# A new order for a four-layer encoder: finer tracking of writes, copies of three heads' outputs, and an earlier guard for the last projection

## The chip, the cores and the metric

The kernel runs on one core of one Trainium2 chip. The metric is device time in microseconds, from the start of the program to its end. It was run three times before the change; the profiled execution is a further one, and its trace shows each instruction on the core's engines: TensorE (PE, with its weight loads PEld), VectorE (DVE), ScalarE (ACT), GpSimd (POOL) and SyncE (SP), which issues the transfers.

## The reference

The program is a trunk of four layers over 512 rows of 1024 channels, all in float32. Each layer normalizes its input, mixes the rows in one of three ways, multiplies by a gate, projects and adds to the input. All mixing is causal by chunks of 64 rows.

```python
for i in range(DEPTH):                     # DEPTH = 4
    kind, j = i % N_MIXERS, i // N_MIXERS  # 0, 1, 2, 0
    h = _rms_norm(x, norm_g[j])
    x = x + mixer[kind](h, ...)

def _diff_attention(h, w_in, ...):         # layers 0 and 3
    q, k, v, gate = jnp.split(h @ w_in, ...)
    # 8 heads; q and k in two maps of 64, normalized and rotated; v of 128
    wts = p[:, :, 0] - lam * p[:, :, 1]    # two softmaxes, chunk-causal
    o = _rms_norm(wts @ v, sub_g) * (1.0 - lambda_init)
    return (o * silu(gate)) @ w_out

def _conformer_conv(h, w_in, ...):         # layer 1
    a, b, gate = jnp.split(h @ w_in + b_in, 3, axis=-1)
    u = a * sigmoid(b)
    u = causal_depthwise_conv(u, conv_w) + conv_b      # 31 taps
    u = silu(_layer_norm(u, ln_g, ln_b))
    return (u * silu(gate)) @ w_out

def _mla(h, w_in, ...):                    # layer 2: latent attention, 8 heads
    ...
    return (o * silu(gate)) @ w_out
```

## The kernel before

**Tiling.** Rows are four tiles of 128, channels eight blocks of 128. A product of full precision is three matmuls: both operands are split in a high and a low part, and the names `Hh`, `Hl` are the two parts of the layer's normalized input. A projection holds accumulators of 128 x 512 in PSUM and runs over eight blocks of the contracted channels, whose weights arrive in four pieces (`g1_w0`, `w2`, `w4`, `w6`). Names begin with the layer (`L0_` to `L3_`; the profile shows `L_` for all): `qk`, `v`, `g` are projections, of which `g0` and `g1` make the two halves of the gate `G`; `h5j2` is head 5, query tile 2, with its scores `sc`, its exponentials `p`, their transposes `wtr` and copies `wt`; `o5` is head 5's output.

**The attention of layers 0 and 3** (`layer_a`). For each head and query tile TensorE makes scores, VectorE their maxima, ScalarE the exponentials; VectorE combines the two maps; TensorE transposes the result and multiplies it with V, into the head's accumulator `po`. Then ScalarE squares the output (`osq`), small operations make the factor of the norm, and `gate_o` (VectorE, L526) multiplies output, factor and gate into `V`. Only after that is `po` free. The gate must have gone through Silu, one ScalarE instruction over 128 x 2048 per half, and Silu and Exp stand in different function tables (`ACT_TABLE_LOAD`). Afterwards `ytr` transposes `V` blockwise, and ScalarE and VectorE split it into the high and low part of `y`.

**The convolution of layer 1** (`layer_b`). Blocks of channels are convolved in two ways. Blocks 0 to 4 run as multiply-and-add steps on VectorE (block 4's are the rows `L1_c4`) or on ScalarE and GpSimd (`cq`, `ct`, `cs`), and TensorE transposes the sums (`ctr`). Blocks 5 to 7 run on TensorE (`L1_c5` to `L1_c7`): `conv_phase` fills a tile `u4` of 128 x 4 x 136 by a memset of margins and sixteen transfers of 32 rows each, and VectorE expands weights (`wa5` to `wa7`, four pieces a block). Then the LayerNorm: statistics of all blocks on VectorE (L547, L550), the root on GpSimd (`lnr_y`, L740), the normalization into `V` (L535), the transposes `ytr`.

**The output projection** (`out_proj`) multiplies `y` with its weights `o0_w`, `o1_w`. In the last layer it begins each accumulator with transposes of the residual `X` (L468 before, L472 after), which a guard, `only_when`, holds back until a named `y` is written.

**What sets the order.** The kernel's methods do not issue instructions. They describe nodes for a planner (class `Plan`), each with an engine, a cost, the buffers it reads and writes, and a place in the program. The planner then simulates the five engines and takes for each the node that could start first; among those that could, the lowest priority number, which is the node's place plus an entry of the table `SHIFT` for its section and engine. It also gives out buffer slots: four for projection accumulators, three for scores and transposes, one for `po` (tag `o`), and in SBUF four of 128 x 512 for scratch (tag `mid`). What depends on what inside the planner is tracked per buffer in grains (`Buf.grain` elements of a row) and parts of the 128 rows (`View.halves`). The order that comes out is issued as it stands, each engine in its own queue, and the waits on the chip are set by the tiles that the instructions touch.

## Time and profile before

| what | value |
|---|---|
| three runs | 1047.22, 1045.62, 1047.05 us (median 1047.05) |
| profiled execution, its own time | 1047.38 us |
| span of its trace | 1045.6 us, 1.8 us less |
| mean granted TensorE clock | 0.99 |
| PE busy | 1006.7 us (96%) |
| DVE busy | 762.4 us (73%) |
| ACT busy | 585.1 us (56%) |
| POOL busy | 194.8 us (19%) |
| DMA | 87.53 MB, mean 84 GB/s |

A row of the slices names the stretch, its length, and each engine's busy time with the number of instructions, then the granted clock of TensorE (1.00 is full speed), the busy share of the DMA engines and GB/s. A row of the waits says which engine waited at which line for what: total, times and longest. A row of the timeline gives start, duration, engine, line and operation, output and inputs, how many instructions of the kind follow one another, and in brackets the idle time ahead of it with what ended it.

### The profile page before, as it was taken

The page shows a single profiled execution, that of the slowest core. Times are in us where ns is not written, and L with a number is a line of the kernel's source. Part 1 is how long each engine was busy: PE and PEld are TensorE (multiplying, and loading weights), DVE is VectorE, ACT ScalarE, POOL GpSimd, SP SyncE. Part 2 cuts the span into 40 slices and gives each one's busy share as a digit, 9 for nine tenths or more (in the row PEclk, how much of TensorE's full clock was granted, in tenths as well). Part 3 has the DMA queues.
Part 4 walks back from the last instruction along what each step waited for, and adds up shares of the span by engine and source line. Part 5 has one row for each costly group of instructions (what it writes and reads, how often), then busy time and mean ns, then how long its engine had stood idle before and what let it go on. Part 6 is the DMA issues. An engine that isn't in the chain of part 4 may idle for free.

```text
span 1045.6 us, 15204 instructions
## 1 busy us (share of the span) xinstructions
PE 1006.7 (96%) x5204; PEld 846.2 (81%) x5204; DVE 762.4 (73%) x1970; ACT 585.1 (56%) x1222; POOL 194.8 (19%) x135
## 2 busy tenths in 40 slices
PE   9999999999999999997999998999999999999798
PEld 7878888787877787886888788788888887887687
DVE  4946899896678999847353869964776589889660
ACT  7437557657444656554343676753526555765742
POOL 3000000000130898950520001000400000000000
PEclk9999999999999999998999999999999999999899
DMA  7343244222124333220232211013325124323002
GB/s 235 93 101 122 61 122 121 66 87 56 41 61 121 122 89 101 66 90 1 73 83 78 71 50 61 22 39 101 119 72 152 38 84 121 102 81 120 22 21 81
DMA packets 74308, 87.53 MB, mean 84 GB/s; under 512 B 17109, under 2 KB 47701, under 8 KB 74232
## 3 DMA queue, kind: packets, MB, share of 16 engines
q1 hardware_dynamic: 74232, 86.57, 28.1%
q8 instruction: 41, 0.67, 0.3%
q14 instruction: 35, 0.29, 0.1%
HBM read 75.28 MB, written 2.10 MB: 74 GB/s over the span
## 4 chain that ended last, share of the span: by engine, by line
PE 72%; DVE 14%; ACT 6%; issue 4%; POOL 2%; DMA 1%; SPq 0%; DVEq 0%; ACTq 0%; POOLq 0%
PE L_o L460 20%; PE L_g_a L460 14%; PE L_qk_a L460 12%; PE L_v_a L460 8%; DVE L_c L526 4%; PE L_ab_a L460 2%; PE L_c_a L460 1%; POOL L_cq L517 1%; PE L_c L460 1%; DVE L_qk_T L514 1%; PE L_qk_tr L466 1%; ACT G L490 1%; PE L_kv_a L460 1%; DVE L_qk_t L514 1%; PE L_h3j_sc L460 1%
## 5 line engine op out<-in xcount | busy, mean ns | idle before, releaser
L460 PE MATMUL L_qk_a<-L_qk_w,Hh 128*128 128x512 f32 x512 | 161.6, 397 | 0.0
L460 PE MATMUL L_o<-L_y,L_o_w 128*128 128x512 f32 x576 | 141.6, 395 | 0.0
L460 PE MATMUL L_g_a<-L_g_w,Hh 128*128 128x512 f32 x384 | 121.4, 397 | 2.3 <-ACT L_qk_sq L490 1.9
L460 PEld LDWEIGHTS L_o<-L_y,L_o_w 128*128 128x128 f32 x576 | 105.2, 188 | 21.1 <-POOL L_o_w L517 0.4
L740 POOL TENSOR_TENSOR L_h_or_y<-L_h_ov,minus_half 128x4 f32<-128x4 f32 x16 | 17.4, 1089 | 484.3 <-DVE L_h_ov L535 311.7
L460 PEld LDWEIGHTS L_qk_a<-L_qk_w,Hh 128*128 128x128 f32 x512 | 92.5, 188 | 16.8 <-ACT G L490 0.3
L460 PE MATMUL L_qk_a<-L_qk_w,Hl 128*128 128x512 f32 x256 | 100.5, 392 | 0.6 <-DVE Hl L526 0.6
L517 POOL TENSOR_TENSOR L_cq<-L_cq,L_ct 128x512 f32<-128x512 f32 x58 | 80.2, 1382 | 27.9 <-DMA L_ab_w_r<-b_w_in 21.3
L460 PE MATMUL L_ab_a<-Hh,L_ab_w 128*128 128x512 f32 x256 | 81.6, 393 | 3.0 <-DVE L_ab_sg L514 2.1
L460 PEld LDWEIGHTS L_g_a<-L_g_w,Hh 128*128 128x128 f32 x384 | 69.6, 188 | 16.6 <-ACT L_qk_sq L490 2.3
L460 PE MATMUL L_v_a<-L_v_w,Hh 128*128 128x512 f32 x256 | 81.0, 397 | 0.7 <-DVE L_qk_t L514 0.5
L460 PE MATMUL L_g_a<-L_g_w,Hl 128*128 128x512 f32 x192 | 75.2, 391 | 0.0
L526 DVE SCALAR_TENSOR_TENSOR L_c<-L_u,L_tab,L_c 128x512 f32<-128x512 f32 x90 | 65.0, 750 | 1.4
L490 ACT ACTIVATE L_ct<-L_u,L_tab 128x512 f32<-128x512 f32 x60 | 42.6, 721 | 33.3 <-POOL L_cq L517 31.6
L460 PEld LDWEIGHTS L_ab_a<-Hh,L_ab_w 128*128 128x128 f32 x256 | 47.9, 188 | 15.4 <-DVE L_ab_sg L514 2.0
L460 PEld LDWEIGHTS L_qk_a<-L_qk_w,Hl 128*128 128x128 f32 x256 | 48.0, 188 | 11.9 <-DVE Hl L526 1.7
L460 PEld LDWEIGHTS L_v_a<-L_v_w,Hh 128*128 128x128 f32 x256 | 46.2, 188 | 9.9 <-DVE L_qk_t L514 1.0
L517 POOL TENSOR_TENSOR L_sqs<-L_sqs,L_sq 128x512 f32<-128x512 f32 x21 | 32.1, 1528 | 98.3 <-ACT L_sq L490 84.5
L514 DVE TENSOR_TENSOR L_g_w<-L_g_w_r,L_g_w 128x1024 fp32r<-128x1024 f32 x32 | 43.9, 1374 | 8.8 <-ACT L_g_w L497 8.2
L460 PE MATMUL L_v_a<-L_v_w,Hl 128*128 128x512 f32 x128 | 50.1, 391 | 0.0
L460 PE MATMUL L_ab_a<-Hl,L_ab_w 128*128 128x512 f32 x128 | 49.9, 390 | 0.0
L497 ACT CAST L_o_w<-L_o_w_r 128x1024 fp32r<-128x1024 f32 x32 | 33.6, 1052 | 28.7 <-PE L_g_a L460 16.4
(368 smaller groups left out, 2313.4 us busy)
## 6 DMA issues: line engine op xcount, KB each, us to landing
L_qk_w_r<-a_w_in SPq DMA_DIRECT2D x62, 256.0 KB, 3.1
L_v_w_r<-a_w_in SPq DMA_DIRECT2D x16, 512.0 KB, 3.8
L_g_w_r<-a_w_in SPq DMA_DIRECT2D x16, 512.0 KB, 3.8
L_qk_st<-L_qk_st SPq DMA_DIRECT2D x32, 256.0 KB, 5.4
L_o_w_r<-a_w_out SPq DMA_DIRECT2D x16, 512.0 KB, 3.5
L_ab_w_r<-b_w_in SPq DMA_DIRECT2D x24, 256.0 KB, 3.1
L_g_w_r<-b_w_in SPq DMA_DIRECT2D x8, 512.0 KB, 3.7
L_o_w_r<-b_w_out SPq DMA_DIRECT2D x8, 512.0 KB, 3.5
```

The source lines that it names most:

```text
L460: lambda nc: nc.tensor.matmul(out.real(), a.real(), b.real(), start=start, stop=stop),
L466: emit = lambda nc: nc.tensor.transpose(out.real(), src.real(), ident.real())
L490: nc.scalar.activation(out.real(), src.real(), func, scale=scale.real() if isinstance(scale, View) else scale, **kw)
L497: lambda nc: nc.scalar.copy(out.real(), src.real()), [src], [out])
L514: lambda nc: nc.vector.tensor_tensor(out=out.real(), in0=a.real(), in1=b.real(), op=op), [a, b], [out])
L517: lambda nc: nc.gpsimd.tensor_tensor(out=out.real(), in0=a.real(), in1=b.real(), op=op), [a, b], [out])
L526: self.add("dve", out.n / 960.0 + (0.13 if isinstance(scalar, View) else 0.068), lambda nc: nc.vector.scalar_tensor_tensor(out=out.real(), ...
L740: self.p.add("pool", 0.32 + 0.18 * v.n, lambda nc: nc.gpsimd.tensor_tensor(out=y.real(), in0=v.real(), in1=self.minus_half[:, 0:v.n].real( ...
```

## The change

1. The planner's tracking is finer. Buffers of 544 elements a row (`u4`) get a grain of 8, those of 1084 (`ub`) a grain of 2, both 32 before; rows are tracked in four parts of 32 in place of two halves of 64.
2. In layers 0 and 3 the outputs of heads 4, 5 and 6 are copied from `po` to a buffer of their own in SBUF (`own`, named `oc`, tag `mid`), four copies a head. Squares and gating read the copy, so `po` is free once it is copied.
3. In the last layer the residual's transposes for the first half of the columns are held back until the y of head 2 is written, not that of head 5; for the second half it stays head 5.
4. The whole table `SHIFT` is replaced, and with it the order on every engine.

```diff
-        self.grain = 1 if size <= 64 else 6 if size == 192 else 32
+        self.grain = 1 if size <= 64 else 6 if size == 192 else 8 if size == 544 else 2 if size == 1084 else 32
...
-        self.writer = [None] * (2 * n)
-        self.readers = [[] for _ in range(2 * n)]
+        self.writer = [None] * (4 * n)
+        self.readers = [[] for _ in range(4 * n)]
...
-            v.halves = tuple(range((rows.start or 0) // 64, -(-(rows.stop or P) // 64)))
+            v.parts = tuple(range((rows.start or 0) // 32, -(-(rows.stop or P) // 32)))
...
-L0_g0_a.act=5733 L0_g0_a.pe=-1495 L0_g0_w.dve=1051 L0_g0_w_r.sp=-99 L0_g1_a.act=4 L0_g1_a.pe=1821 L0_g1_w.act=-392
...
+L1_c7.pe=-2941 L1_cq1.act=-499 L1_cq1.pool=-2768 L1_cq3.act=105 L1_cq3.pool=-7916 L1_cs0.act=-118 L1_cs1.pool=-7781
...
-        return 0.115 if len(out.halves) == 1 and out.n > 256 else 0.0
+        return 0.115 if len(out.parts) <= 2 and out.n > 256 else 0.0
...
-                    with p.only_when(reads=(y[5][0],)), p.group("pe"):
+                    with p.only_when(reads=(y[5 if c else 2][0],)), p.group("pe"):
...
             sq = self.buf("mid", N + "_osq")
+            if 4 <= h < 7:
+                own = self.buf("mid", N + "_oc", [P, NT, P])
+                for jb in range(NT):
+                    p.copy(own[:, jb, :], po[:, jb, :])
+                po = own
             for jb in range(NT):
                 p.act(sq[:, jb * P:(jb + 1) * P], po[:, jb, :], AF.Square, accum=ss[:, jb:jb + 1])
```

The numbers of instructions are the same on PE, DVE, POOL and SP; ACT has 24 more, the copies. Where the order is changed is shown at three places. Rows give line, operation, output and inputs, shape and count.

**TensorE, end of layer 1, before.** From the gate's last matmuls (`L1_g1_a3`) over the turns `ctr` and block 7 (`L1_c7`) to the transposes of the normalized rows (`ytr`):

```order
L460 MATMUL L1_g1_a3_4296<-Hh_115,L1_g1_w6_4280 128x512
L466 MATMUL L1_ctr2_4519<-ident_109,L1_cs2_4084 128x128 x4
L466 MATMUL L1_ctr4_4527<-ident_109,L1_cs4_4329 128x128 x4
L466 MATMUL L1_ctr3_4549<-ident_109,L1_cs3_4532 128x128 x4
L460 MATMUL L1_c7_4379<-L1_wa7_0_4371,L1_u47_4380 128x128 x9
L460 MATMUL L1_c7_4379<-L1_wa7_1_4382,L1_u47_4380 128x128 x9
L460 MATMUL L1_c7_4379<-L1_wa7_2_4583,L1_u47_4380 128x128 x9
L460 MATMUL L1_c7_4379<-L1_wa7_3_4595,L1_u47_4380 128x128 x9
L466 MATMUL L1_ctr1_4606<-ident_109,L1_cs1_4035 128x128 x4
L466 MATMUL L1_ytr1_4639<-ident_109,V_117 128x128 x4
L466 MATMUL L1_ytr3_4647<-ident_109,V_117 128x128 x4
L466 MATMUL L1_ytr0_4655<-ident_109,V_117 128x128 x4
```

All of this stands behind the gate.

**TensorE, the same place, after.** Block 7, behind the first part of the gate's matmuls:

```order
L464 MATMUL L1_g1_a3_4447<-Hh_115,L1_g1_w0_4224 128x512
L464 MATMUL L1_c7_4274<-L1_wa7_0_4298,L1_u47_4275 128x128 x9
L464 MATMUL L1_c7_4274<-L1_wa7_1_4311,L1_u47_4275 128x128 x9
L464 MATMUL L1_c7_4274<-L1_wa7_2_4480,L1_u47_4275 128x128 x9
L464 MATMUL L1_c7_4274<-L1_wa7_3_4494,L1_u47_4275 128x128 x9
L470 MATMUL L1_ctr3_4507<-ident_109,L1_cs3_4482 128x128 x4
L470 MATMUL L1_ctr4_4514<-ident_109,L1_cs4_4465 128x128 x4
L464 MATMUL L1_g1_a3_4447<-Hh_115,L1_g1_w0_4224 128x512
L464 MATMUL L1_g1_a3_4447<-Hl_116,L1_g1_w0_4224 128x512
L464 MATMUL L1_g1_a3_4447<-Hh_115,L1_g1_w0_4224 128x512
```

And the first transposes, 45 matmuls of the gate later:

```order
L464 MATMUL L1_g1_a3_4447<-Hl_116,L1_g1_w4_4356 128x512
L464 MATMUL L1_g1_a3_4447<-Hh_115,L1_g1_w4_4356 128x512
L470 MATMUL L1_ytr1_4604<-ident_109,V_117 128x128 x4
L470 MATMUL L1_ytr0_4613<-ident_109,V_117 128x128 x4
L470 MATMUL L1_ytr2_4619<-ident_109,V_117 128x128 x4
L464 MATMUL L1_g1_a0_4396<-Hh_115,L1_g1_w6_4401 128x512
L464 MATMUL L1_g1_a0_4396<-Hl_116,L1_g1_w6_4401 128x512
L464 MATMUL L1_g1_a0_4396<-Hh_115,L1_g1_w6_4401 128x512
L470 MATMUL L1_ytr3_4635<-ident_109,V_117 128x128 x4
L464 MATMUL L1_g1_a1_4410<-Hh_115,L1_g1_w6_4401 128x512
```

Block 7 and two turns moved from behind the gate into its first third, and seven of the eight transposes between its last matmuls; `ctr1` and `ctr2` come earlier still.

**VectorE, layer 1, before.** Ahead of the memset of block 7's input (`L1_u47`):

```order
L526 SCALAR_TENSOR_TENSOR L1_c4_3799<-L1_u2_3242,L1_tab_2536,L1_c4_3799 128x512 x3
L514 TENSOR_TENSOR L1_wa6_2_4340<-L1_d4_3314,wx_112 128x1152
L514 TENSOR_TENSOR L1_wa6_3_4357<-L1_d4_3314,wx_112 128x1152
L514 TENSOR_TENSOR L1_wa7_0_4371<-L1_d4_3314,wx_112 128x1152
L553 MEMSET L1_u47_4380 128x4x8
L514 TENSOR_TENSOR L1_wa7_1_4382<-L1_d4_3314,wx_112 128x1152
L514 TENSOR_TENSOR V_117<-L1_c6_4120,cb_113 128x128 x2
L547 BN_STATS L1_stat_3774<-V_117 128x6 x2
```

**VectorE, the same place, after.**

```order
L518 TENSOR_TENSOR G_118<-L1_g0_a2_4191,L1_tab_2417 128x512
L530 SCALAR_TENSOR_TENSOR L1_c4_3906<-L1_u2_3261,L1_tab_2417,L1_c4_3906 128x512
L518 TENSOR_TENSOR G_118<-L1_g0_a3_4208,L1_tab_2417 128x512
L530 SCALAR_TENSOR_TENSOR L1_c4_3906<-L1_u2_3261,L1_tab_2417,L1_c4_3906 128x512
L557 MEMSET L1_u47_4275 128x4x8
L530 SCALAR_TENSOR_TENSOR L1_c4_3906<-L1_u2_3261,L1_tab_2417,L1_c4_3906 128x512
L518 TENSOR_TENSOR L1_wa7_2_4480<-L1_d4_3307,wx_112 128x1152
L518 TENSOR_TENSOR L1_wa7_3_4494<-L1_d4_3307,wx_112 128x1152
L518 TENSOR_TENSOR V_117<-L1_c7_4274,cb_113 128x128 x2
L551 BN_STATS L1_stat_3843<-V_117 128x6 x2
L518 TENSOR_TENSOR V_117<-L1_c7_4274,cb_113 128x128 x2
```

The memset now stands among the last steps of block 4, behind the second weight piece of block 7 and behind block 6's additions and statistics; the other two weight pieces and block 7's additions follow directly.

**TensorE, layer 3, before.** The gate's last matmuls and head 5's products with V (`L3_o5`):

```order
L460 MATMUL L3_g1_a3_9253<-L3_g1_w6_9202,Hh_115 128x512 x2
L460 MATMUL L3_g1_a3_9253<-L3_g1_w6_9202,Hl_116 128x512
L460 MATMUL L3_h5j3_sc0_9441<-L3_qk2_st1_8805 128x512 x2
L460 MATMUL L3_h5j3_sc1_9446<-L3_qk2_st1_8805 128x512 x2
L466 MATMUL L3_ytr1_9452<-ident_109,V_117 128x128 x4
L466 MATMUL L3_ytr3_9466<-ident_109,V_117 128x128 x4
L460 MATMUL L3_o5_9482<-V_117,L3_h5j0_wt_9169 128x128
L460 MATMUL L3_o5_9482<-V_117,L3_h5j1_wt_9424 128x128 x2
L466 MATMUL L3_h5j2_wtr_9487<-ident_109,L3_h5j2_p_9178 128x128 x3
L466 MATMUL L3_ytr2_9497<-ident_109,V_117 128x128 x4
L460 MATMUL L3_h6j0_sc0_9509<-L3_qk3_st0_9268 128x256 x2
```

**TensorE, layer 3, after.** Head 5's first products, behind the gate's first accumulator, with three quarters of the gate still to come:

```order
L464 MATMUL L3_g1_a0_9252<-L3_g1_w6_9256,Hh_115 128x512 x2
L464 MATMUL L3_g1_a0_9252<-L3_g1_w6_9256,Hl_116 128x512
L464 MATMUL L3_o5_9301<-V_117,L3_h5j0_wt_9159 128x128
L464 MATMUL L3_o5_9301<-V_117,L3_h5j1_wt_9216 128x128 x2
L470 MATMUL L3_h5j2_wtr_9308<-ident_109,L3_h5j2_p_9169 128x128 x3
L464 MATMUL L3_g1_a1_9316<-L3_g1_w0_8928,Hh_115 128x512 x2
L464 MATMUL L3_g1_a1_9316<-L3_g1_w0_8928,Hl_116 128x512
```

And what stands behind the gate's last matmul:

```order
L464 MATMUL L3_g1_a3_9359<-L3_g1_w6_9256,Hl_116 128x512
L464 MATMUL L3_h6j1_sc1_9564<-L3_qk3_st0_9406 128x256 x2
L470 MATMUL L3_ytr0_9569<-ident_109,V_117 128x128 x4
L464 MATMUL L3_o5_9301<-V_117,L3_h5j2_wt_9309 128x128 x3
L464 MATMUL L3_o5_9301<-V_117,L3_h5j3_wt_9422 128x128 x4
L470 MATMUL L3_h6j0_wtr_9593<-ident_109,L3_h6j0_p_9518 128x128
L472 MATMUL L3_o03_9595<-ident_109,X_111 128x128 x4
L464 MATMUL L3_h6j2_sc0_9607<-L3_qk3_st0_9406 128x384 x2
L464 MATMUL L3_o6_9611<-V_117,L3_h6j0_wt_9592 128x128
L464 MATMUL L3_o01_9531<-L3_o0_w0_9369,L3_y0_9468 128x512 x3
L464 MATMUL L3_h6j2_sc1_9624<-L3_qk3_st0_9406 128x384 x2
```

Head 5's first products moved from behind the gate's last matmul to behind its first accumulator; scores of head 6 and the residual's transposes (`L3_o03` here, the other three ahead) now lie there too. On ScalarE the copies of heads 4 and 5 stand ahead of the Silu of this half of the gate.

## The prediction

> **What bounds the kernel now.** I read the page, then the span in slices of 10 us, then TensorE's waits, and last the timeline of the slices that stand out.

> ```profile
> PE 1006.7 (96%) x5204; PEld 846.2 (81%) x5204; DVE 762.4 (73%) x1970; ACT 585.1 (56%) x1222; POOL 194.8 (19%) x135
> core 0: us, PE busy (x) PEld busy (x) DVE busy (x) ACT busy (x) POOL busy (x), PEclk, DMA share, GB/s
> 200.00:210.00 10.00, 8.10 (x44) 6.55 (x42) 8.78 (x30) 7.29 (x22) 1.01 (x1) 1.00 0.20 68
> 240.00:250.00 10.00, 8.26 (x49) 7.52 (x49) 3.63 (x17) 8.27 (x22) 0.00 (x0) 0.83 0.17 54
> ...
> 440.00:450.00 10.00, 10.00 (x57) 8.67 (x56) 4.25 (x11) 7.59 (x10) 9.69 (x7) 1.00 0.06 14
> 450.00:460.00 10.00, 10.00 (x46) 8.29 (x45) 1.75 (x3) 4.99 (x8) 6.42 (x4) 1.00 0.41 124
> 460.00:470.00 10.00, 7.94 (x57) 7.64 (x56) 8.46 (x22) 4.12 (x7) 3.58 (x2) 0.83 0.30 101
> 470.00:480.00 10.00, 4.96 (x39) 4.23 (x37) 6.17 (x22) 0.59 (x1) 1.02 (x1) 0.87 0.00 1
> 480.00:490.00 10.00, 9.01 (x44) 7.48 (x44) 9.91 (x18) 8.80 (x14) 0.00 (x0) 0.79 0.01 2
> 870.00:880.00 10.00, 8.11 (x39) 6.46 (x38) 7.83 (x28) 6.11 (x12) 0.00 (x0) 1.00 0.62 150
> 960.00:970.00 10.00, 7.05 (x37) 5.35 (x35) 8.75 (x17) 9.63 (x14) 1.01 (x1) 0.95 0.70 198
> 970.00:980.00 10.00, 7.97 (x42) 6.90 (x42) 6.46 (x26) 8.46 (x25) 0.00 (x0) 0.71 0.04 14
> 980.00:990.00 10.00, 8.70 (x52) 6.50 (x51) 8.20 (x32) 6.75 (x20) 1.01 (x1) 1.00 0.01 2
> ```

> TensorE is busy for 1006.7 of 1045.6 us and idle for 38.9. Its instructions stay the same in kind and number, so only idle time and withheld clock can be won; the other engines matter where TensorE waits for them. In each row PE's busy time follows the comma, and the granted clock is the third number from the right. Of all slices only six have a clock under 1, at three places. The idle time is 10 us less the busy time; the clock's loss is what is missing from 1, times 10 us (a little high, since idle time is in it).

> - End of layer 0's attention, 240 to 250: 1.7 idle and 1.7 clock, 3.4 us.
> - End of layer 1's convolution, 460 to 490: 2.1 + 5.0 + 1.0 idle and 1.7 + 1.3 + 2.1 clock, 13.2 us.
> - End of layer 3's attention, 960 to 990: 3.0 + 2.0 + 1.3 idle and 0.5 + 2.9 clock, 9.7 us.

> Together 26.3 us. At 200 and at 870 TensorE is idle for 1.9 us with the clock at 1.00, so one gap of that size costs only itself. [...]

> ```profile
> PE L_ytr L466 <- DVE V L535: 5.0, 1, 5.0
> PE L_o L460 <- DVE V L526: 4.6, 2, 2.8
> PE L_ctr L466 <- ACT V L497: 2.1, 1, 2.1
> PE L_g_a L460 <- ACT L_qk_sq L490: 1.9, 1, 1.9
> ```

> The longest wait is layer 1's LayerNorm; the second, met twice, is a product of weights with V behind the gating of the head before.

> **Layer 1: the convolution moves ahead.** The timeline before:

> ```profile
> 460.09 1.04 PE L466 MATMUL L_ctr<-ident,L_cs 128*128 128x128 f32 x8
> 460.84 1.28 POOL L517 TENSOR_TENSOR L_cs<-L_cq,L_ct 128x512 f32<-128x512 f32 x1 [2.47 <-PE L_ctr L466]
> 462.07 2.36 POOL L517 TENSOR_TENSOR L_o_w<-L_o_w_r,L_o_w 128x1024 fp32r<-128x1024 f32 x1
> 463.65 9.83 PE L460 MATMUL L_c<-L_wa,L_u 128*128 128x128 f32 x72
> 473.32 0.60 PE L466 MATMUL L_ctr<-ident,L_cs 128*128 128x128 f32 x4
> ...
> 475.90 1.04 DVE L550 BATCH_NORM_AGGREGATE L_mv<-L_stat 128x2 f32<-128x48 f32 x4
> 478.28 3.74 DVE L535 TENSOR_SCALAR V<-V,L_mv,L_lnr_y 128x512 f32<-128x512 f32 x8 [1.13 <-POOL L_lnr_y L740]
> 478.97 5.77 PE L466 MATMUL L_ytr<-ident,V 128*128 128x128 f32 x24 [5.04 <-DVE V L535]
> ```

> The gate's last matmul ends at 460.09. TensorE then turns conv outputs, runs block 7's convolution (72 records) and has nothing while VectorE and GpSimd make the LayerNorm: 478.97 - 473.32 = 5.65 us from the last turn to the first transpose of y. The new order puts block 7 behind 27 of the 96 gate matmuls, 45 more of them between it and the first transpose of y, and the last 24 among those transposes.

> ```profile
> 425.43 0.39 PE L460 MATMUL L_g_a<-Hl,L_g_w 128*128 128x512 f32 x1
> 426.11 0.39 PE L460 MATMUL L_g_a<-Hl,L_g_w 128*128 128x512 f32 x1
> ...
> 440.56 1.36 DVE L514 TENSOR_TENSOR L_wa<-L_d,wx 128x1152 f32<-128x1152 f32 x1 [0.94 <-PE L_c L460]
> 442.60 0.09 DVE L553 MEMSET L_u<- 128x32 f32 x1 [0.69 <-PE L_c L460]
> 460.90 1.67 DVE L547 BATCH_NORM_STATS2 L_stat<-L_ctr 128x6 f32<-128x128 f32 x8
> ```

> Three gate matmuls take 426.11 - 425.43 = 0.68 us, so 0.227 each. Cover: the two turns (1.04 us for eight records, as at 460.09) and 45 x 0.227 = 10.2 make 11.2 us of TensorE work behind block 7. The chain it covers is 5.65 us and eight more statistics (0.21 each by the row at 460.90), 6.5 us with a step more. So 4.7 us are spare, if block 7 itself is on time. TensorE comes to it at 460.09 - 69 x 0.227 + 0.9 (two turns now done earlier) = 445.3. What it needs last is the clearing of its input's margins on VectorE, which in the trace came at 442.60 behind a wait for TensorE. Ahead of it VectorE now also has one more weight expansion (1.36, as at 440.56), four additions (some 0.24 each, an estimate by the statistics) and twelve statistics (2.5), less one conv step (0.7): 4.1, less the 0.94 + 0.69 that it idled just before: 445.1. The turn behind block 7 needs a sum from GpSimd. There GpSimd was free at 460.84 - 2.47 = 458.4, and three weight casts (2.36 each) now stand behind that sum: 451.3, with its 1.28 us 452.6. TensorE gets there at 445.3 and some 9 us of block 7, 454. Both are level with need, so a wait of 0 to 4 us is in it.

> VectorE has room behind it: 5.8 and 8.3 us idle in the slices at 440 and 450, and four gate products and the next layer's tables now stand behind the LayerNorm. Whoever is late next is the first output projection, through the y of the blocks that need the gate's last columns. I leave 2.5 us of the 13.2: **10.7 us** saved, between 6 (4 us of wait and two clock losses of 1.7, as at 240) and 13. On GpSimd one of the three casts stands ahead of the LayerNorm's root, the others behind it, 10 us before their use.

> **Layers 3 and 0: the attention output leaves PSUM early.** There is one accumulator for a head's output. Head 5's products wait until head 4's gating has read it, and that waits for the Silu of the gate:

> ```profile
> 967.33 1.28 ACT L490 ACT_TABLE_LOAD   x1
> 968.62 1.91 ACT L490 ACTIVATE G<-G 128x2048 f32<-128x2048 f32 x1
> 970.56 1.13 DVE L526 SCALAR_TENSOR_TENSOR V<-L_o,L_h_or_y,G 128x128 f32<-128x128 f32 x4 [1.27 <-ACT G L490]
> 971.74 1.65 PE L460 MATMUL L_o<-V,L_h5j_wt 128*128 128x128 f32 x6 [2.84 <-DVE V L526]
> ...
> 242.21 1.65 PE L460 MATMUL L_o<-V,L_h5j_wt 128*128 128x128 f32 x6 [1.74 <-DVE V L526]
> 980.31 0.26 ACT L497 COPY L_h6j_wt<-L_h6j_wtr 128x128 f32<-128x128 f32 x1
> ```

> The change adds 24 copies of 128x128 from PSUM, all on ScalarE. The last row is a copy of that shape from PSUM, 0.26 us, so 24 x 0.26 = 6.2 us of ScalarE. Below: nothing, where ScalarE idles (it is busy for 56% of the span by the page). Above: the whole 12 of layer 3, 3.1 us, where it is the bound; in the slices at 960 and 970 it is busy for 18.1 of 20 us. I take 1 us, inside the remainders below.

> What they buy in layer 3: head 5's first products stand right behind the first gate column, its later scores and turns inside the gate's matmuls, and with the new guard the residual's transposes of three accumulators too. Behind the gate's last matmul the first instruction that needs the Silu is the transpose of head 4's y. Ahead of it stand 20 rows, 10.8 us: 28 matmuls of 512 columns at 0.227 make 6.4, and products, turns and smaller scores some 4.4, an estimate by their sizes. In the trace the Silu ended 970.53 - 964.86 = 5.7 us behind the gate's last matmul; ScalarE now has some 3.5 us more of copies, squares and exponentials ahead of it (seven pieces of 0.28 to 0.7), and the gating takes 1.13: 10.3 us. Level again, so 0 to 3 us stay, for the second table load (1.28) behind the Silu too. I leave 1.7 of 9.7: **8.0 us**, between 5 and 9.7.

> ```profile
> 964.86 1.10 PE L460 MATMUL L_h5j_sc<-L_qk_st 128*128 128x512 f32 x4
> ```

> In layer 0 head 5's products end inside the gate's matmuls, and of the 3.4 us I leave 0.7: **2.7 us**, between 0 and 3.4.

> **The rest.** Every queue is in a new order, and 38.9 - 16.1 = 22.8 us of idle time lie elsewhere in pieces of 2 us or less. Nothing in them favours a sign: 0, between -4 and +5. Finer tracking adds no instruction; the waits on the chip come from the tiles themselves. SP sends the conv inputs of a block in one run instead of in pieces, ahead of the projection's weights; those are needed 10 us later, so I take nothing.

> **Sum.** 10.7 + 8.0 + 2.7 = 21.4. The profiled execution took 1047.38, so 1026.0; the median of the three runs is 0.3 lower, so I say **1026 us**.

> **Rivals.**

> 1. *Half of it.* The two level races are lost: in layer 1 block 7 waits for VectorE and two clock losses of 1.7 stay (4 + 3.4 - 2.5 = 5 us), in layer 3 ScalarE is late with Silu and exponentials and one stays (3 + 1.7 - 1.7 = 3 us), and the rest costs 4. 1026 + 12 = 1038. For: both come out within 1 us. Against: each needs several rows to slip.

> 2. *It doesn't do what it says.* The accumulator is free only once ScalarE, in order, has reached the copies; if these stand behind what waits for the same gate, head 5 is as late as before, and layer 1's chain is as long when VectorE is the limit. 1047. Against: head 5's copies stand ahead of the Silu in the new order.

> 3. *Slower: VectorE falls behind in layer 1.* It is busy for 88.5 of the 90 us from 330 to 420 (row below). By the two orders block 5's convolution now comes 8.4 us of TensorE work earlier, block 6's 12.1 and block 7's 16.1. If VectorE can't be earlier, TensorE idles 16.1 us in three pieces, and with four clock losses of 1.7 (6.8) loses 22.9 us more there: 1049. From 21.4 on, the sum of the savings, the change is slower. Against: ahead of block 5's last weights VectorE has ten conv steps fewer (six took 4.03 us), so it is earlier too.

> ```profile
> 404.82 4.03 DVE L526 SCALAR_TENSOR_TENSOR L_c<-L_u,L_tab,L_c 128x512 f32<-128x512 f32 x6
> 330.00:420.00 90.00, 86.35 (x411) 70.46 (x410) 88.51 (x130) 49.75 (x67) 72.93 (x48) 1.00 0.36 102
> ```

> **How the numbers follow.** The forecast 0.64 (1018 to 1033), rival 1 0.22, rival 2 0.06, rival 3 0.08. A measurement tells this kernel from no change at about 0.2%, 2 us. Faster: 0.64 + 0.22 = 0.86; same 0.06; slower 0.08. For the range I leave out the slow rivals and what lies under the forecast's end: 1015 to 1041. The lower end is all three places won (26.3) and 5 us elsewhere; the upper one is rival 1 and 3 us.

> **What would show it.** In the profile after, the wait of the transposes for V and that of head 5's products for the gating are gone or under 2 us; the clock is 1.00 in all but one or two slices; TensorE's idle time falls to about 23 us. Block 7's convolution should lie before the gate's end with no wait ahead of it. I am wrong if TensorE waits at the convolutions of blocks 5 to 7 (rival 3), if the head's products still wait for gating (rival 2), or if idle time of the same size turns up in layers 0 to 2 where I counted nothing.

## The result and the profile after

The changed kernel takes **1014.94 us** (median of four runs, 1011.72 to 1015.68) against 1047.13 for the kernel before beside it: ratio 0.9689, 95% interval 0.9665 to 0.9712, 32 us less. The forecast was 1026 in a range from 1015 to 1041: the sign is right, the gain is half as large again as forecast, and the time lies just outside the range, 0.06 us below its lower end. That is far less than the 4 us by which the four runs differ. The profiled execution took 1015.47, its span is 1013.7.

The first line of the page, and then TensorE's longest waits:

```profile
PE 994.4 (98%) x5204; PEld 840.5 (83%) x5204; DVE 769.2 (76%) x1970; ACT 589.4 (58%) x1246; POOL 195.5 (19%) x135
...
PE L_h2j_sc L464 <- DMA L_qk_st<-L_qk_st: 2.2, 2, 1.5
PE L_h6j_sc L464 <- DMA L_qk_st<-L_qk_st: 1.9, 1, 1.9
PE L_o L464 <- DVE L_y L518: 1.3, 1, 1.3
```

TensorE is idle for 1013.7 - 994.4 = 19.3 us, 38.9 before. The two longest waits of before, for layer 1's `V` and for the gating ahead of head 5, are gone. The longest now are for moves of q and k inside SBUF. The slices of 10 us at the places that the forecast named, and the only two places before the last slice that show a clock under 1:

```profile
230.00:240.00 10.00, 8.14 (x46) 6.28 (x45) 6.18 (x15) 7.33 (x15) 0.00 (x0) 0.93 0.99 237
240.00:250.00 10.00, 10.00 (x47) 8.43 (x47) 6.47 (x23) 9.49 (x19) 0.00 (x0) 0.90 0.19 65
...
450.00:460.00 10.00, 10.00 (x59) 8.45 (x58) 8.21 (x10) 4.79 (x6) 5.85 (x4) 1.00 0.31 106
460.00:470.00 10.00, 8.67 (x43) 6.87 (x42) 10.00 (x15) 9.05 (x14) 2.39 (x1) 1.00 0.19 58
...
840.00:850.00 10.00, 7.80 (x38) 6.41 (x37) 7.82 (x13) 4.95 (x9) 0.00 (x0) 0.97 0.93 221
850.00:860.00 10.00, 10.00 (x49) 8.77 (x48) 8.04 (x33) 5.08 (x14) 1.41 (x1) 0.85 0.17 42
...
950.00:960.00 10.00, 9.98 (x56) 8.31 (x56) 7.95 (x30) 9.91 (x24) 1.23 (x1) 1.00 0.17 54
960.00:970.00 10.00, 10.00 (x68) 8.64 (x68) 7.38 (x28) 7.07 (x27) 0.00 (x0) 1.00 0.00 0
```

Counted as in the prediction, idle time and clock together: the end of layer 1 went from 13.2 us to 1.3 (the idle time at 460), the end of layer 3 from 9.7 to nothing, the end of layer 0 from 3.4 to 3.6. There the wait for the gating is gone and a wait of 1.86 us for a move stands in its place, with the DMA engines at 0.99. Together 21.4 us are saved. That this is the very sum of the forecast is luck: layer 1 gave 1.2 us more than forecast, layer 3 gave 1.7 more and layer 0 gave 2.9 less. The other 10.5 us lie in what it had put at nothing.

**Where they are.** Two points can be found in both traces at which the same matmuls have been done: the last product of layer 1's input projections (397.6 before, 388.7 after) and the first product of layer 2 (530.7, 510.2). The stretches between them, before and then after:

```profile
0.00:397.60 397.60, 387.16 (x1908) 320.12 (x1908) 314.68 (x789) 230.64 (x475) 82.77 (x59) 1.00 0.35 100
397.60:530.70 133.10, 123.46 (x648) 104.91 (x649) 88.79 (x147) 68.68 (x97) 77.52 (x51) 0.96 0.20 60
530.70:1045.60 514.90, 496.09 (x2649) 421.18 (x2647) 358.91 (x1036) 285.79 (x650) 34.50 (x27) 0.99 0.26 77
```

```profile
0.00:388.70 388.70, 383.32 (x1910) 319.16 (x1911) 314.52 (x788) 234.04 (x488) 82.11 (x59) 1.00 0.35 102
388.70:510.20 121.50, 118.21 (x649) 100.36 (x647) 93.55 (x148) 68.29 (x96) 77.62 (x51) 1.00 0.22 67
510.20:1013.70 503.50, 492.81 (x2649) 421.00 (x2647) 361.12 (x1037) 287.11 (x663) 35.82 (x26) 1.00 0.27 79
```

| stretch | forecast | saved | idle time | clock | neither |
|---|---|---|---|---|---|
| layer 0 and the input projections of layer 1 | 2.7 | 8.9 | 5.1 | 0.0 | 3.8 |
| the rest of layer 1 | 10.7 | 11.6 | 6.4 | 5.1 | 0.1 |
| layers 2 and 3 | 8.0 | 11.4 | 8.1 | 1.6 | 1.7 |
| sum | 21.4 | 31.9 | 19.6 | 6.7 | 5.6 |

Idle time is a stretch's length less PE's first number; the clock is summed over the slices below 1. In the first stretch no single stall stands out. By the waits, six of 0.6 to 2.1 us are gone or shorter (for squares of q and k 1.9, for the gating 1.7, for the sigmoids of layer 1's inputs 2.1 to 0.6, for a weight tile 0.9, for the input `x` 0.8, for `Hl` 0.6), and two are new, for the move (1.9) and for `Hh` (1.2). The named stall of layer 0 costs 0.2 us more than before, so this stretch gave 9.1 of the 10.5 us; layers 2 and 3 gave 1.7 beyond the named stall there, and the rest of layer 1 gave -0.3.

The last column is time in which TensorE counts as busy in both. Part of it lies at the start, in a slice that gives a clock of 1.00 in both. Matmuls of 128 columns on a tile of ones (`L_warm`), before and then after:

```profile
6.47 2.34 PE L460 MATMUL L_warm<-ones 128*128 128x128 f32 x10
```

```profile
6.33 1.55 PE L464 MATMUL L_warm<-ones 128*128 128x128 f32 x12
```

They take 0.23 us each before and 0.13 after, at nearly the same time; why is not shown. The first projection begins at 10.88 us before and at 9.88 after. At least part of this 1.0 us is not the new order's doing: a variant below has the order of before up to layer 1 (block 7 moved in the kernel before), and its first projection begins at 9.77. With the changed kernel's order at the start it begins anywhere from 8.87 (coarse tracking, below) to 9.88.

Most of the remainder is small gaps. In the rows at 425.43 and 426.11 that the prediction shows, a product of 512 columns lasts 0.39 us though the next starts 0.227 behind it, so a gap of up to 0.16 us can't be seen as idle. The starts in the two traces bear this out: from 12 us on and outside the stretches of half clock, matmuls that start over 0.02 us later than the median for their shape hold 32.7 us of time that counts as busy before, and 28.3 after. What held each of them back is not shown.

**Layer 1 and layer 3 in the timeline.** The clearing of block 7's margins on VectorE, block 7 and the first transposes of y on TensorE, with the first four of the eight pieces of the normalization on VectorE and a weight cast on GpSimd:

```profile
436.37 0.09 DVE L557 MEMSET L_u<- 128x32 f32 x1
436.72 8.20 PE L464 MATMUL L_c<-L_wa,L_u 128*128 128x128 f32 x72
444.75 1.04 PE L470 MATMUL L_ctr<-ident,L_cs 128*128 128x128 f32 x8
445.55 0.48 PE L464 MATMUL L_g_a<-Hh,L_g_w 128*128 128x512 f32 x1
451.20 4.12 DVE L539 TENSOR_SCALAR V<-V,L_mv,L_lnr_y 128x512 f32<-128x512 f32 x4 [1.13 <-POOL L_lnr_y L744]
451.74 2.39 POOL L521 TENSOR_TENSOR L_o_w<-L_o_w_r,L_o_w 128x1024 fp32r<-128x1024 f32 x1 [0.57 <-ACT L_o_w L501]
455.85 1.47 PE L470 MATMUL L_ytr<-ident,V 128*128 128x128 f32 x12
```

TensorE doesn't wait. The margins are clear at 436.46, 0.3 us before block 7 begins. GpSimd's sum for the turn behind block 7 is done at 441.15, 3.6 us ahead of that turn. From the last turn to the first transpose TensorE now has 455.85 - 445.55 = 10.3 us of gate matmuls (10.2 forecast).

The first piece of `V` is done at 451.75, 4.1 us ahead of the first transpose (4.7 forecast). But a block's four transposes read one piece for each of the four row tiles. The fourth piece is done only at 451.20 + 4.12 = 455.32, and its transpose starts at 456.17: 0.85 us are spare. In the kernel before the same four pieces took 1.92 us; here the second alone took 2.74, while the cast ran on GpSimd. No run tests whether the cast is the cause.

In layer 3, the gate's last matmul, the Silu, the gating of heads 4 and 5 and the transpose that needs head 4's:

```profile
948.34 0.40 PE L464 MATMUL L_g_a<-L_g_w,Hl 128*128 128x512 f32 x1
955.52 1.92 ACT L494 ACTIVATE G<-G 128x2048 f32<-128x2048 f32 x1
957.47 2.19 DVE L530 SCALAR_TENSOR_TENSOR V<-L_h_oc,L_h_or_y,G 128x128 f32<-128x128 f32 x8
959.82 0.66 PE L470 MATMUL L_ytr<-ident,V 128*128 128x128 f32 x4
```

The Silu ends 957.44 - 948.74 = 8.7 us behind the gate (9.2 forecast), head 4's gating 1.1 later, at 958.6; the transpose comes 11.1 us behind the gate (10.8 forecast). That race was won by 1.2 us.

### The profile page after: what moved, and what is told of

The parts are those of the page before. It is cut to its first block, busy times and chain, and to the rows that moved or that the text cites. A ratio compares the mean times of both kernels' runs of the same rounds, so it can differ in the third digit from the quotient of the medians.

```text
span 1013.7 us, 15192 instructions
## 1 busy us (share of the span) xinstructions
PE 994.4 (98%) x5204; PEld 840.5 (83%) x5204; DVE 769.2 (76%) x1970; ACT 589.4 (58%) x1246; POOL 195.5 (19%) x135
## 4 chain that ended last, share of the span: by engine, by line
PE 79%; DVE 10%; ACT 4%; POOL 3%; DMA 2%; issue 2%; SPq 0%; DVEq 0%; ACTq 0%; POOLq 0%
PE L_o L464 22%; PE L_g_a L464 14%; PE L_qk_a L464 14%; PE L_v_a L464 7%; PE L_ab_a L464 4%; PE L_c L464 2%; PE L_c_a L464 2%; POOL L_cq L521 2%; DVE L_c L530 1%; DMA L_qk_st<-L_qk_st 1%; PE L_qk_tr L470 1%; PE L_h6j_sc L464 1%; DVE L_qk_st L518 1%; PE L_ytr L470 1%; DVE L_qk_T L518 1%
## 5 line engine op out<-in xcount | busy, mean ns | idle before, releaser
L464 PEld LDWEIGHTS L_o<-L_y,L_o_w 128*128 128x128 f32 x576 | 106.2, 189 | 22.9 <-DVE L_y L518 1.8
L464 PEld LDWEIGHTS L_ab_a<-Hh,L_ab_w 128*128 128x128 f32 x256 | 48.0, 188 | 11.4 <-ACT L_ct L494 1.0
L518 DVE TENSOR_TENSOR L_qk_w<-L_qk_w_r,L_qk_w 128x1024 fp32r<-128x1024 f32 (+1 forms) x30 | 36.5, 1219 | 22.3 <-ACT L_qk_w L501 22.1
L464 PE MATMUL L_o<-L_o_w,L_y 128*128 128x512 f32 (+1 forms) x216 | 49.6, 373 | 0.0
```

The costliest lines, as they stand in the source:

```text
L464: lambda nc: nc.tensor.matmul(out.real(), a.real(), b.real(), start=start, stop=stop),
L518: lambda nc: nc.vector.tensor_tensor(out=out.real(), in0=a.real(), in1=b.real(), op=op), [a, b], [out])
```

## The experiments

Every variant was timed beside the kernel before, whose median lay between 1045.7 and 1047.4 in all of these; differences are given against the changed kernel's 1014.9. Its own four runs lie from 1011.7 to 1015.7, so a difference of some 2 us tells nothing. Most variants keep an order that the planner has made and move a few named rows in it. The shorthand `late=[(what, behind)]` puts the nodes of `what` just behind the last node of `behind` on the planner's list; whatever depends on them follows, and all else stays. `early` puts nodes, with all that they need, just behind a numbered node; a node of the gate is three matmuls.

### The convolution of layer 1

Block 7 goes back behind the gate, as before; the rest of the changed order stays.

```diff
 plan.order()
+plan.resort(late=[(at("pe", "L1_c7"), has("pe", "L1_g1_a\d"))])
```

> The changed kernel with its order frozen, and one thing put back: block 7's convolution in layer 1 stands behind the gate's last matmul again, with what depends on it; every other instruction keeps its place. Theory A (each of the three stalls was worth its idle time and its withheld clock): the 13.2 us of the old stall return less the 1.3 that are left in the changed kernel, so 1015 + 12 = 1027 us, between 1024 and 1030, with slices under a clock of 1.00 around 455 to 485. Rival B (the new order as a whole hides the chain, wherever block 7 stands): 1015 to 1019.

Measured: 1028.91 us (1027.73 to 1031.04), ratio 0.9829 [0.9812, 0.9846], 14.0 slower, inside theory A's range. The waits and the slices:

```profile
PE L_ytr L478 <- DVE V L547: 4.7, 1, 4.7
PE L_ctr L478 <- POOL L_cs L529: 4.3, 1, 4.3
...
430.00:440.00 10.00, 5.12 (x22) 3.60 (x21) 5.88 (x9) 6.69 (x10) 9.37 (x7) 1.00 0.15 52
...
460.00:470.00 10.00, 6.33 (x57) 6.13 (x55) 5.51 (x15) 0.00 (x0) 0.73 (x1) 1.00 0.00 0
470.00:480.00 10.00, 6.70 (x30) 4.73 (x31) 8.37 (x16) 6.27 (x11) 0.28 (x1) 0.83 0.01 2
```

The wait for `V` is back at nearly its old length (5.0 before), and a turn that had stood behind block 7 now waits 4.3 us for GpSimd. So the place of block 7 is worth the whole stall at the end of layer 1. That it cost 14.0 us and not the 11.9 that the two traces show is a difference near the noise; the 4.3 us for GpSimd are a wait that the kernel before did not have.

The opposite: the kernel before, with block 7 behind 27 of the gate's matmuls and seven of the eight transposes of y behind 72.

```diff
 plan.order()
+plan.resort(early=[(at("pe", "L1_c7"), has("pe", r"L1_g1_a\d"), 8),
+                   (has("pe", r"L1_ytr[0123467]"), has("pe", r"L1_g1_a\d"), 23)])
```

> The kernel before with its order frozen, and one thing moved: in layer 1 block 7's convolution stands behind 27 of the gate's 96 matmuls, the turns and the first transposes of y behind 72, each with all that it needs. Theory A: most of the 13.2 us go, 8 to 12, so 1035 to 1039 us. Rival C (VectorE or GpSimd can't deliver earlier in the old order, so TensorE waits in the middle of the gate instead): 1043 to 1048 us.

Measured: 1064.26 us (1060.99 to 1067.4), ratio 1.0164 [1.0136, 1.0192]: 17 us slower than the kernel before, outside the ranges of both theories. The wait for `V` became 6.2 us and one of the first output product for the last y came in, 6.8 us:

```profile
476.74 6.51 PE L474 MATMUL L_ytr<-ident,V 128*128 128x128 f32 x28 [6.16 <-DVE V L543]
...
497.68 0.79 PE L468 MATMUL L_o<-L_y,L_o_w 128*128 128x512 f32 x1 [6.84 <-ACT L_y L505]
```

In this edit two turns had stayed directly ahead of the transposes, at 469.23, so that the chain from the turns to `V` had no cover at all, and the last y had too few gate matmuls ahead of the product that needs it. That is a flaw of the edit and says nothing of what the move can win. It does show that moving block 7 buys nothing when no cover stands between the last turn and the first transpose, and again between the transposes and the first output product. The move with its full cover was not tried in the old order.

### The copies

In layer 3 and in layer 0 the twelve copies are left out. Squares and gating of heads 4 to 6 read the accumulator in PSUM again, so the next head's products stand behind the gating of the head before.

```diff
+for b in own: b.alias = po["L3_o" + b.name[4]]     # oc is the accumulator itself
+for n in plan.nodes:
+    if has("act", r"L3_h[456]_oc")(n): n.emit = []
+plan.resort(late=[(at("pe", f"L3_o{h + 1}"), at("dve", f"L3_h{h}_oc")) for h in (4, 5, 6)])
```

> The changed kernel with its order frozen, but in layer 3 the squares and the gating of heads 4 to 6 read the accumulator in PSUM again, the 12 copies are left out, and the products of heads 5, 6 and 7 stand behind the gating of the head before, as the one accumulator demands. Theory A: the stall behind the Silu returns, 6 to 10 us, so 1021 to 1025 us, with a wait of head 5's products for the gating near 950. Rival B (the earlier guard and the order of the rest fill the gap): 1015 to 1018.

> The changed kernel in its own order with the 12 copies of layer 0 left out: square, factor and gating of heads 4 to 6 read the accumulator in PSUM, so the products of heads 5 to 7 stand behind the gating of the head before. Theory A (the copies are what lets the order hide the Silu in layer 0 too; a DMA wait merely stands in the same place): 6 to 20 us slower, 1021 to 1035, with waits of the products for V. Rival (the copies of layer 0 are worth what the stall of the kernel before cost, 3.4 us, or nothing): 1015 to 1018.5.

Measured: without layer 3's, 1044.02 us (1038.89 to 1045.3), ratio 0.996 [0.9943, 0.9977], 29 slower; without layer 0's, 1037.1 us (1036.18 to 1041.91), ratio 0.9917 [0.9891, 0.9942], 22 slower. Both theories on layer 3 were far too low; layer 0 came out 2 us above theory A. The longest wait of the first, and slices of the first and then of the second:

```profile
PE L_o L472 <- DVE V L538: 8.4, 2, 6.1
...
940.00:950.00 10.00, 5.18 (x25) 3.96 (x23) 4.58 (x5) 8.28 (x9) 0.00 (x0) 0.92 0.49 150
950.00:960.00 10.00, 4.63 (x17) 3.43 (x17) 2.38 (x6) 2.97 (x9) 0.00 (x0) 0.50 0.02 8
960.00:970.00 10.00, 7.73 (x36) 6.72 (x36) 4.38 (x18) 4.68 (x10) 0.00 (x0) 0.55 0.21 54
```

```profile
240.00:250.00 10.00, 4.67 (x21) 3.25 (x21) 1.83 (x3) 4.48 (x11) 0.00 (x0) 0.56 0.00 0
250.00:260.00 10.00, 7.00 (x29) 5.64 (x30) 4.80 (x19) 7.05 (x15) 0.00 (x0) 0.50 0.22 54
```

From 940 to 990 layer 3 now has 17.1 us of idle time and 12.0 of withheld clock, which is the 29; from 230 to 300 layer 0 has 15.3 and 15.4, against 3.6 together in the changed kernel (its profiled run was the slowest of the four, 27 us over the changed kernel's). In the kernel before the same wait for the gating cost 9.7 at the end of layer 3. The likely reason is that the new order has put heads 5 and 6, the gate and the last projection into one another, so that more hangs on each wait; an order made anew without the copies was not tried. This answers the term for layer 0: its copies are worth 22 us to this order, although the place that the forecast counted there shows no gain.

All 24 copies issued twice, in the unchanged order:

```diff
+if has("act", r"L[03]_h[456]_oc")(n): n.emit = n.emit * 2
```

> The changed kernel in its own order; each of the 24 copies of the head outputs out of PSUM is issued twice, so ScalarE has 24 more copies of 0.26 us (6.2 us). Theory A (the copies lie in ScalarE's idle time): no more than 1 us slower, 1014.9 to 1016. Rival (ScalarE sets the end of layer 3, where it is busy for over nine tenths of the slices): the twelve of layer 3 count in full, 3.1 us, 1018.

Measured: 1016.74 us (1016.0 to 1017.32), ratio 0.9712 [0.9698, 0.9727], 1.8 slower, between the two theories. 24 copies more are 6.4 us of ScalarE by their 0.267 us each in this profile, so at most a part of it reaches the end. The intervals of this ratio and of the changed kernel's overlap, so 1.8 us is hardly told from nothing. The forecast had taken 1 us for the first 24.

### The guard and the finer tracking

Both were taken back in the planner's dependences alone: the changed order stays, and only a node that the old rule makes dependent is moved.

```diff
-with p.only_when(reads=(y[5 if c else 2][0],)), p.group("pe"):
+with p.only_when(reads=(y[5][0],)), p.group("pe"):
```

> The changed kernel in its own order, except that the last projection's first half is guarded by the y of head 5 again: 16 transposes of the residual (0.12 us each) and 27 products of 512 columns (0.227 us each), 8 us of TensorE work, stand behind the transposes of head 5's y instead of ahead of them. Theory A (in layer 3 the guard gives the cover that hides the Silu and the heads 5 and 6, the copies only make room): TensorE idles for 4 to 8 us of it, and one or two clock losses of 1.7 come on top, 1020 to 1026. Rival (the copies alone carry layer 3): at most 2 us slower, 1015 to 1017.

Measured: 1022.26 us (1019.51 to 1023.07), ratio 0.9761 [0.9745, 0.9776], 7.3 slower, as theory A expected. The slice with the loss, and the longest wait in it:

```profile
950.00:960.00 10.00, 5.93 (x26) 4.64 (x26) 7.73 (x33) 9.61 (x23) 1.23 (x1) 0.71 0.17 54
...
955.94 1.22 PE L467 MATMUL L_h6j_sc<-L_qk_st 128*128 128x512 f32 x2 [2.65 <-ACT L_h6j_wt L504]
```

Without the 8 us of products TensorE runs ahead of ScalarE, which is busy for 9.61 of the 10 us, and waits for head 6's copies and exponentials. So in layer 3 the copies make room and the guard fills it; this order needs both.

```diff
-self.grain = ... else 8 if size == 544 else 2 if size == 1084 else 32
+self.grain = ... else 32                            # and rows in two halves
```

> The changed kernel in its own order, except where the coarse tracking of the kernel before (grains of 32 elements, halves of the 128 rows) puts a node behind one that it does not depend on with the fine tracking: the clearing of the margins of four conv inputs comes in two pieces instead of one, the second piece just ahead of the use, and 12 of 16 moves into the inputs of block 5 and of block 7 stand two or three rows later on SP; nothing else moves. Theory A (the finer tracking is worth little by itself, the order was only found with it): 0 to 2 us slower, 1015 to 1017. Rival (the moves of blocks 5 and 7 come late and TensorE waits for its convolutions): 3 to 6 us slower, 1018 to 1021.

Measured: 1015.12 us (1013.5 to 1016.35), ratio 0.9696 [0.9682, 0.9711], 0.2 from the changed kernel, which is no difference. The finer tracking is worth nothing by itself that these runs can tell; whether the table could have been found without it stays open.

### The move that took the gating's place

On SP, the weight loads of the projection that stand ahead of the moves of q and k go behind them.

```diff
+plan.resort(late=[(at("sp", "L0_o0_w6_r", "L0_o1_w0_r"), at("sp", "L0_qk3_st0", "L0_qk3_st1")),
+                  (at("sp", "L3_v1_w6_r", "L3_qk3_w0_r"), at("sp", "L3_qk1_st0", "L3_qk1_st1"))])
```

> The changed kernel with four weight transfers moved on SyncE's queue alone: two in layer 0 and two in layer 3 stand behind the transfers that shift the queries and keys of the next heads, not ahead of them. In the changed kernel TensorE waits for these shifts 1.9 us at 237 and 2.2 us at 848, and the clock is under 1.00 in the slices behind. Theory D (the shifts wait in the DMA engines behind 1 MB of weights): both waits go or halve, and the clock's loss of 1.7 us at each place with them, 1015 - 4 to 7 = 1008 to 1011 us. Rival E (the shifts' own 1 MB sets the time, or the weights are late instead): 1013 to 1017 us.

Measured: 1013.14 us (1012.09 to 1013.9), ratio 0.9675 [0.9661, 0.969], inside the rival's range and not theory D's. Layer 0's wait and its clock loss are gone; in layer 3 the load of the value weights now comes late, ScalarE is idle for 4.21 us ahead of its cast, and TensorE waits 3.53 us for the square that ScalarE does behind that:

```profile
845.61 1.04 ACT L509 CAST L_v_w<-L_v_w_r 128x1024 fp32r<-128x1024 f32 x1 [4.21 <-DMA L_v_w_r<-a_w_in]
846.97 1.28 PE L472 MATMUL L_o<-V,L_h1j_wt 128*128 128x128 f32 x8 [3.53 <-ACT L_h_osq L502]
```

The value weights' load was put back, and only the next projection's load (`L3_qk3_w0_r`) left behind the moves.

> The changed kernel in its own order; on SP two weight loads of layer 0's projection stand behind the moves that head 6 waits for, and in layer 3 the first load of the first projection's weights stands behind the moves that head 2 waits for; the load of the value weights stays where it is (it was moved too in the run before, and ScalarE then waited 4.2 us for it). Theory A (a move of q and k lands late because it queues behind weight loads in the DMA engines, and its wait brings a clock loss): both waits and both clock losses go, 3.5 + 1.8 to 4 us, so 1009 to 1011. Rival (the load of the projection's weights is itself needed early in layer 3, so a wait takes the place of a wait): only layer 0's part stays, 1011.5 to 1013.

Measured: **1008.55 us** (1007.75 to 1010.03), ratio 0.9632 [0.9616, 0.9648]. It is the fastest version, 6.4 us under the changed kernel, with both waits and both clock losses gone. How long a move took to land in layer 0, in the changed kernel and in this one:

```profile
DMA to landing us min/median/max: 7.0/7.2/7.4
```

```profile
DMA to landing us min/median/max: 3.2/4.0/4.6
```

In layer 3 it went from 7.9 to 3.3 us. The moves are the same, four of 256 KB each. What differs in layer 0 is whether two loads of 512 KB were issued just ahead of them. In layer 3 two loads of 256 KB went behind them, and the value weights' 512 KB stayed ahead, issued 1.9 us before the first move.

### The order, layer by layer

The changed code with the whole old table, and with the old entries for one layer (the planner makes a new order from them):

```diff
 SHIFT = ...   # entries of before: all, or those of one layer
```

> The changed code (finer tracking, copies, the guard of head 2) with the kernel before's table of shifts, so that the planner makes an order of its own. Theory A (the gain lies in an order that uses the new freedom, and the table carries it): no gain over the kernel before, 1040 to 1065. Rival (the freedom alone carries it, whatever the table): 1015 to 1030.

> The changed code with the changed table, except that the entries of layer 1 are those of the kernel before; the planner's order of the other layers stays as it is but for a few rows at the borders. Theory A (the new order of layer 1 wins more than the stall at its end, in small waits of its projections and its convolution): at least 16 us slower, 1030 to 1045. Rival (layer 1 gives the stall at its end and nothing else): as with the late convolution, 12 to 15 us, 1027 to 1030.

> The changed code with the changed table, except that the entries of layer 2 are those of the kernel before; no copy, no guard and no stall of the forecast lies in layer 2. Theory A (what the forecast put at nothing, the rest, was won by the order in every layer): 2 to 10 us slower, 1017 to 1025. Rival (layer 2 has no part in the gain): within 1 us, 1014 to 1016.

Then the old entries' order for the nodes of one layer, spliced into the changed order of the others:

> The changed kernel, layers 1 to 3 in its own order; the work of layer 0 in the order that the planner makes of the changed code with the old entries for layer 0. Theory A (what the forecast put at nothing lies mostly in layer 0: by the two traces the last product of layer 1's input projections ends 8.9 us earlier, with the same work done): 6 to 11 us slower, 1021 to 1026. Rival (layer 0 gives nothing, as its stall is merely replaced, and the 8.9 us belong to the border with layer 1): at most 2 us slower, 1015 to 1017.

> The changed kernel, layers 0, 2 and 3 in its own order; the work of layer 1 in the order that the planner makes of the changed code with the old entries for layer 1. Theory A (by the two traces 11.6 us lie between layer 1's input projections and its end, all of it the stall at the end; the 35 us of the run with the old table came from a border that the planner made anew): 12 to 15 us slower, 1027 to 1030. Rival (the old order of layer 1 does not fit the new one around it, border or not): 25 to 36 us slower, 1040 to 1051.

> The changed kernel, layers 0 to 2 in its own order; the work of layer 3 in the order that the planner makes of the changed code with the old entries for layer 3. Theory A (by the two traces layer 3 gives 7 to 8 us): 7 to 12 us slower, 1022 to 1027. Rival (copies and guard alone, in any order, take the stall away): at most 3 us slower, 1015 to 1018.

And the order that a layer has in the kernel before, row for row, spliced in the same way:

```diff
+at[node] = place in the order of before      if node is of the layer
+at[node] = place in the changed order        otherwise
```

> The changed kernel with one layer taken from the kernel before: all the work of layer 1 in the very order that it has there, layers 0, 2 and 3 in the changed kernel's order (a handful of rows at the borders apart). Theory A (the gains of the layers add up, and the two traces share them out: 11.6 us between layer 1's input projections and its end): 11 to 14 us slower, 1026 to 1029. Rival (the orders of the layers lean on one another, as the planner's runs with one layer's old entries seemed to say): over 18 us slower, above 1033.

> The changed kernel with all the work of layer 2 in the very order that it has in the kernel before. Theory A (the two traces give layer 2 about 4 us, though the change has no copy, no guard and no stall there): 2 to 5 us slower, 1017 to 1020. Rival (what the forecast put at nothing is noise or lies at the borders): within 1 us, 1014 to 1016.

> The changed kernel with all the work of layer 3 in the very order that it has in the kernel before, without the twelve copies of layer 3. Theory A (the two traces give layer 3 about 7.5 us): 7 to 10 us slower, 1022 to 1025, with the waits of products for V that the kernel before has. Rival (the copies are worth the 29 us that leaving them out of the new order cost): over 18 us slower, above 1033.

| kernel | median us | ratio [interval] | against the changed kernel |
|---|---|---|---|
| whole old table | 1097.73 | 1.049 [1.0467, 1.0514] | +82.8 |
| old table, layer 1 | 1050.5 | 1.0037 [1.0023, 1.0052] | +35.6 |
| old table, layer 2 | 1016.99 | 0.9716 [0.9701, 0.973] | +2.1 |
| old table's order, layer 0 | 1052.16 | 1.0051 [1.0033, 1.0069] | +37.2 |
| old table's order, layer 1 | 1039.67 | 0.993 [0.9911, 0.995] | +24.7 |
| old table's order, layer 3 | 1041.45 | 0.9958 [0.9943, 0.9974] | +26.5 |
| layer 1 as before | 1043.36 | 0.9972 [0.9954, 0.9989] | +28.4 |
| layer 2 as before | 1028.57 | 0.982 [0.9788, 0.9852] | +13.6 |
| layer 3 as before | 1043.7 | 0.9969 [0.9954, 0.9984] | +28.8 |

The whole old table with the new code is 83 us slower than the changed kernel and 50 slower than the kernel before, beyond even theory A's range; so the freedom alone carries nothing, and the gain lies in the order. The theory that the layers' gains add up fell. Three layers as before cost 70.8 us together, though all four gained 32, and for layers 1 and 3 the rivals' ranges held. Only layer 2 with its old entries came near what theory A said, and its 2.1 us are hardly clear of the noise. The profile shows why the costs don't add up, for layer 1 as before:

```profile
290.00:300.00 10.00, 6.21 (x16) 4.16 (x15) 5.91 (x8) 2.33 (x4) 3.38 (x2) 0.66 0.20 56
300.00:310.00 10.00, 7.13 (x31) 5.34 (x29) 3.98 (x6) 3.73 (x6) 1.15 (x1) 1.00 0.26 75
310.00:320.00 10.00, 9.28 (x29) 7.47 (x29) 2.86 (x5) 2.37 (x4) 3.02 (x3) 0.66 0.10 26
...
470.00:480.00 10.00, 10.00 (x77) 10.00 (x76) 3.60 (x6) 0.73 (x2) 1.03 (x1) 0.83 0.15 52
480.00:490.00 10.00, 4.96 (x23) 3.98 (x22) 8.62 (x28) 2.89 (x5) 1.02 (x1) 0.70 0.01 2
```

From 460 to 500 idle time and clock add up to 13.2 us, the stall of the kernel before to a tenth. Another 14.2 us lie from 290 to 320, where layer 0 ends and layer 1 begins: there the two orders meet that were not made for one another. Layer 3 as before loses 10.2 us at its border (710 to 740) and 21.3 at its end, where before it lost 9.7; why that stall doubled is not settled. So these runs confirm the stall at the end of layer 1. They do not tell how much of the 8.9 us ahead of it belongs to which row of layer 0, and that stays open.

## Why the prediction was right, and where it was not

**Layer 1, 10.7 us: right, mechanism and size.** 11.9 us by the slices, 14.0 by taking the move back. The cover came out at 11.1 us (11.2 forecast). The chain to the first piece of `V` took 7.0 us, not 6.5; the forecast's own terms, 5.65 and eight statistics of 0.21, add up to 7.3, so its 6.5 is a slip in the sum. It also ended the chain at the first piece, where the first block needs four: of the 4.7 us that it called spare, 0.85 were left.

Of the two races that were called level, the one with VectorE was just that: 0.3 us apart, 0.2 in the forecast. TensorE reached block 7 at 436.7, not 445.3, mostly because it came 8.9 us earlier out of layer 0, and VectorE came as much earlier with it. The race with GpSimd was won by 3.6 us. So that nothing waits here was a near thing twice, and in part luck. The 2.5 us left for the first output projection were 1.3.

**Layer 3, 8.0 us: right in mechanism, a little low.** 9.7 were won. The race of Silu and transpose was forecast at 10.3 against 10.8 us and run at 9.8 against 11.1. The 1.7 us left for the second table load and for ScalarE never came. That the guard is part of the cover was in the forecast as one clause; the run puts it at 7.3 us.

**Layer 0, 2.7 us: wrong as a place.** Its stall was taken away as described and its time went to a transfer: the moves for head 6 were issued behind two weight loads and landed 7.2 us after their issue. The forecast had read the order on SP only for layer 1. It did not ask what would be late next in the DMA engines.

**The rest, 0 between -4 and +5: the step that failed.** It gave 10.5 us: 6.7 of idle time and the 5.6 that is neither idle time nor clock in the views, less 1.8 of clock at 840. Of these, 9.1 lie in layer 0 and the input projections of layer 1, and up to 1.0 of the 9.1 is the first projection's earlier start, 9.88 against 10.88 us, at least part of which is luck. The reasoning was that every queue is in a new order and nothing favours a sign. But 22.8 us of idle time were known to lie there in small waits, so more than 5 could be won; the bounds of -4 and +5 were worked out from no row. They were too narrow on both sides: other orders of the same code lie from 6 us below this one to 83 above. With 10 us for this term the lower end of the range would have been near 1011, not 1015. Which rows of layer 0 won the time stays open, since no run takes that apart.

**The copies, 1 us: not contradicted.** Issued twice, they cost 1.8 us more, at the edge of the noise; what the first 24 cost was not measured apart.

**Rivals.** None came: no wait for VectorE above 0.2 us at blocks 5 to 7, no products behind the gating, no half of the gain. The signs named in advance held but for two: TensorE's idle time is 19.3, below the 23 expected, and the clock is under 1 in four slices, not two.

## What to carry to other kernels

When a change replaces the order of everything, the named stalls give a good sum for themselves, but the term for all the other waits must be bounded by the idle time that lies there, not by a few microseconds. A stall that is covered again must be followed to the transfers too: read on the issuing queue what stands ahead of each move that a freed engine will ask for next. Where a chain ends in several pieces, the race is decided by the last one that is needed. And what a part of a finely packed order costs when it is taken back is not what it saved: the copies cost 29 us against a stall of 9.7 in layer 3 and 22 against 3.4 in layer 0, two fifths to a half of it by the clock.

## What the runs showed of the hardware

**Where stalls lay close together, the clock stayed down between them.** Without the copies of layer 3 TensorE worked at 0.50 and 0.55 through two slices in which it was busy for 4.6 and 7.7 us; 12.0 of the 29 us were clock. A forecast of this stall by its idle time alone would have been short by 40%.

```profile
613.98:617.39 3.41, 2.52 (x21) 2.18 (x18) 3.40 (x12) 0.99 (x3) 0.00 (x0) 1.00 0.45 154
617.39:620.81 3.42, 2.72 (x14) 2.31 (x14) 3.11 (x15) 1.29 (x5) 0.00 (x0) 1.00 0.00 0
```

```profile
614.98:618.39 3.41, 1.83 (x13) 1.43 (x12) 3.40 (x14) 0.58 (x4) 0.00 (x0) 1.00 0.50 159
618.39:621.81 3.42, 3.42 (x11) 2.95 (x12) 2.39 (x12) 0.77 (x3) 0.00 (x0) 0.50 0.00 0
```

In the first the two larger gaps fall into two steps, TensorE is busy for 2.52 and 2.72 us of them, and the clock stays. In the second both fall into one step, TensorE is busy for 1.83 of 3.41 us, and the next step runs at 0.50. In the fastest it is the same, with 1.81 us. So here the clock was lost behind steps in which TensorE was busy for 1.83 and 1.81 of 3.41 us. The same order met the steps at different places in these runs, and a forecast of it would have had to price the two gaps with and without the 1.7 us.

**A move inside SBUF landed later behind weight loads.** Moves of 256 KB took 7.2 us to land behind two loads of 512 KB and 4.0 us ahead of them (medians of four), with the DMA engines at 0.99 and 0.85 in the slice from 230 to 240. Only the issue order on one queue was changed between the two.
